# RWKV-7 chunk preparation: decay sums and head sums as products on the tensor engine instead of a scan and split operands

## The chip, the cores and the metric

The kernel runs on one core of a Trainium2 chip. The metric is the device time of one execution in microseconds (us), as the median of several runs. The engines are named as in the profile: PE is the tensor engine (PEld its weight loads), DVE the vector engine, ACT the scalar engine, POOL the general-purpose engine (GpSimd), and SP the engine whose queue issues most of the transfers.

## The reference, cut to what matters

The reference is a trunk of two layers on 1024 positions of 1024 channels, all in float32. The first layer (RG-LRU and HGRN2 beside each other) isn't touched. The second is RWKV-7 time mixing with 16 heads of 64 channels:

```
r, k, v, g = einsum("pbsd,pdw->pbsw", mixes[:4], w_in)
w_log = -softplus(-(w0 + tanh(mixes[4] @ w1) @ w2)) - 0.5
decay = exp(-exp(w_log))
iclr  = sigmoid(a0 + (mixes[5] @ a1) @ a2)
kk = heads(k * k_k);  kk = kk / max(norm(kk), 1e-12)
k  = heads(k * (1 + (iclr - 1) * k_a))
# step: state = state * w + (state @ -kk) (kk * iclr)^T + v k^T ;  y = state @ r
bonus = sum(r * k * r_k, axis=-1) * v
```

Two things of this matter here. The exponent of the decay is -exp(-0.5) times a sigmoid, so the decay over several positions is the exponential of a running sum of sigmoids. And two sums go over the 64 channels of a head: the squared norm of `kk`, and the sum of `r * k * r_k`.

## The kernel before, in words

The kernel works on the second layer in chunks of 64 positions. In a chunk the recurrence becomes products of matrices and the inverse of a triangular matrix of 64 x 64 per head. Three stages follow one another in time.

**Preparation** (`layer1_proj` from line 942 on, and `prep`, line 1144). The keys' projection runs over four units of weights (j), two halves of the positions (th, 512 each) and two column tiles of 128 channels (e2): sixteen slots, in the order of line 961. In each slot `dense_t` (lines 152 to 165) makes 24 products of 512 columns into a PSUM tile "mm". A generator `prep` for the same channels and half runs in three steps, one slot apart:

1. Two products per factor (lines 1152 to 1157) give the low-rank parts of decay and rate, channels on partitions, in PSUM tiles "l", of which there are two buffers. ACT takes the tanh of both (SG and IC, lines 1160 and 1161; the decay's constant w0 is the bias). DVE adds 1 (line 1166) and makes the running sum GC inside each chunk with a scan whose first factor `cst` is 0 at the start of a chunk (line 1167). ACT makes E1 and E2, the exponentials of plus and minus the sum (lines 1172 and 1174); E2 lies in the tile of SG. POOL makes the right half of AR (line 1176).
2. With the projected keys: KP and the square SQ, the scaled keys KK (lines 1181 to 1183); `head_sums` of SQ (line 1185) and of RK, which is r times k times r_k (line 1192); BT (line 1188), the left half of AR (line 1189) and KTt, which lies in the tile of GC (line 1194).
3. Sixteen small products (line 1201) into a tile "s", copied by ACT to AB (line 1205), and eleven transfers on SP's queue: AR, BT, KTt and AB to DRAM (lines 1206 to 1217).

`head_sums` (lines 1219 to 1228) splits its operand into two float32r parts (the high one by ACT, line 149; the low one by DVE, line 150) and multiplies both with a selector of 64 columns that puts the two heads' sums into their rows of one PSUM tile `nb` of 64 x 512, in which all the slots add. After the last slot `norms` (line 1230) copies `nb`, transposes the bonuses' part, and inverts the norms, on 32 partitions by 512 columns (line 1241); they go to DRAM in eight transfers (line 1245) and come back in two (line 1256), with 32 positions to a row.

**Values and inversions** (`chain_phase`, line 1023). The value pieces (`vpiece`, lines 1000 to 1011; their 24 products of 256 columns are lines 184 to 186) run on PE, six of them still before `chain_phase`; their mixes are made at the same time in the tiles "KK" of the preparation. The inversions (`invert`, line 1264) are long rows of small DVE steps (lines 1294 to 1306), which begin with a block of AB's products scaled by the inverse norms (lines 1275 to 1279, on POOL).

**The chunks** one after another (`gram`, `chain`, `norm`, `project`), with the other inversions, the gates and the output among them.

The order of the instructions on each engine isn't written out by hand. The program issues its steps in the order of the code above, and a scheduler that simulates the timeline when the kernel is built arranges them by priority and simulated readiness; each engine then runs its list in that order. Tiles of one name (or tag) share a fixed number of buffers, and a write waits for the last reader of the buffer's earlier tile.

Of the kernel before, what the change touches and what calls it, by code (L numbers as in the profile page):

```python
# [11 lines left out]
ALU = mybir.AluOpType  # L12
# [13 lines left out]
# columns of the packed per-channel vectors, eight columns each  # L26
# [6 lines left out]
class Steps:  # L33
    """a generator with the parts that it makes"""
# [11 lines left out]
class Net:  # L46
# [39 lines left out]
    # ---------------------------------------------------------------- constants  # L86
# [15 lines left out]
    def mask_from(self, pool, tmp, name, shape, conds):  # L102
        """uint8 mask, 1 where every affine condition (pattern, base, cm) >= 0 holds."""
# [48 lines left out]
    def dense_t2(self, w, e, uh, ul, th):  # L152
        """[128 channels, 512 positions] of unit w's e-th column tile, in two steps."""
# [21 lines left out]
    def dense_n(self, w, uh, ul, tt):  # L175
        """[128 positions, 256 channels] of unit w."""
# [12 lines left out]
    def rstd(self, pool, ss, n, scale, eps):  # L189
        """(ss * scale + eps) ** -0.5 on [128, n]."""  # L190
# [6 lines left out]
    def rstd2(self, pool, ss, n, scale, eps):  # L197
        """the same by the square root of the scalar engine and a Newton step"""
# [10 lines left out]
    def norm_rows(self, pool, x, sq):  # L209
        """root-mean-square scale [128,1] of a row tile [128, 1024]."""  # L210
        nc = self.nc
        ss = pool.tile([P, 1], F32, name="ss")
        nc.scalar.activation(sq, x, AF.Square, accum_out=ss)
        return self.rstd(pool, ss, 1, 1.0 / D, EPS)

    # ---------------------------------------------------------------- layer 0
    def layer0(self):
        tc, nc, a = self.tc, self.nc, self.a
        with ExitStack() as cx:
            uh, ul = ([[self.mx.tile([P, HALF], F32R, name=f"x{n}{th}") for _ in range(KT)] for th in range(2)] for n in "hl")  # L220
            rgk = cx.enter_context(self.pool("rgk", 1))
            with ExitStack() as c2:
# [38 lines left out]
                # the first projections of the next part lie in PSUM until its pools are there  # L261
# [17 lines left out]
    def warm(self, pool, n):  # L279
        """products of zeros that keep the tensor engine's clock up until there is work"""  # L280
# [9 lines left out]
    def hgrn_consts(self, c, hp):  # L290
        nc = self.nc
        # lower bound and its complement, per channel
# [16 lines left out]
        # masks of a 64-block's rows and columns, the same in both halves of the partitions  # L309
# [6 lines left out]
        # (block, group of blocks, source block of a group)  # L316
# [9 lines left out]
    def hgrn_dense(self, c, big, uh, ul, trees):  # L326
        """the projections, in pieces; a tree starts when its queries and keys are there"""
# [61 lines left out]
    def advance(self, gens):  # L389
        """a stage of the first tree, at times one of the second too"""  # L390
# [5 lines left out]
    def hgrn_half(self, hp, stp, th, j, tr, st, diag, lev):  # L396
        """two heads, four blocks of 128 positions each; the heads run in step"""
        nc = self.nc
        # scores, transposed
# [3 lines left out]
        def scores(i, rhs, w, n, b):  # L403
            """products of the sources of a block of 64 with its groups of n blocks of b targets, w blocks apart"""
# [9 lines left out]
        def put(i, ps, w, b, g, s, mask, dst, src):  # L414
            """the blocks dst of every group of g from the slots src of every w, where the mask allows it"""
# [9 lines left out]
        def wider(i, b, pool):  # L425
            """sources with their way through the other half of a block of 2 * b, totals of such blocks"""
# [8 lines left out]
        # positions themselves and next ones  # L435
# [17 lines left out]
        # blocks of 4 * b from such of b: the slots of a group are queries of its blocks 0 to 3 (even ones) and those of  # L453
        # blocks 2, 3, 3 with their ways through block 1, blocks 1 and 2, block 2 (odd ones)
# [57 lines left out]
        for Q, F, K, V, G, row in tr:  # L512
            # keys with positions on partitions
# [72 lines left out]
    def rglru(self, cx, uh, ul):  # L586
        tc, nc, a = self.tc, self.nc, self.a
        # -8 softplus(-lam) per channel: max(-lam, 0) + log1p(exp(-|lam|))
# [19 lines left out]
        # sigmoids by tanh: sigmoid(z) = (1 + tanh(z / 2)) / 2  # L608
# [11 lines left out]
        for j in range(4):  # L620
# [45 lines left out]
            # the halves of the two sigmoids that are factors, squared  # L666
# [10 lines left out]
    def out0(self, cx):  # L677
# [9 lines left out]
        for th in range(2):  # L687
# [69 lines left out]
    def finish(self, rp, th, Y, ss):  # L757
        """norms and residual of four row tiles, and their channels on partitions"""
# [29 lines left out]
    def receptance(self, w, j, th, e2):  # L788
        """a column tile of r, in two steps"""
# [15 lines left out]
    def mix_parts(self, mp, p, th, eng=None):  # L805
        """the same, a channel tile at a step"""
# [13 lines left out]
    def mixes(self, mp, p, th, eng=None):  # L820
        """the parts of one half of a mix, in the slots of that half"""
# [8 lines left out]
    def lora_consts(self):  # L830
        """the first factors of decay and rate, times 1 - mu and times mu"""
# [16 lines left out]
    def lora(self, th):  # L848
        """low-rank decay and rate of one half"""
# [18 lines left out]
    def lora_parts(self, th, x):  # L868
        """the low parts of the decays on the second half of the partitions, those of the rates on the first"""
# [7 lines left out]
    def layer1_consts(self):  # L877
# [6 lines left out]
        # halves for sigmoids by tanh: 1 + (sigmoid - 1) k_a = tanh * k_a / 2 + 1 - k_a / 2  # L884
        cols = lambda n: self.vec[:, VIDX[n]:VIDX[n] + KT]
        self.hw0, self.ha0, self.hka, self.omka = (c.tile([P, KT], F32, name=n) for n in ("hw0", "ha0", "hka", "omka"))
        nc.vector.tensor_scalar(self.hw0, cols("w0"), 0.5, None, ALU.mult)
# [4 lines left out]
    def layer1_proj(self):  # L892
# [7 lines left out]
        self.ddd = dt("ddd", [4, 16, 8, 32])  # L900
# [4 lines left out]
        with ExitStack() as cx:  # L905
            mp = self.mx
            with ExitStack() as c2:
                lp = c2.enter_context(self.pool("lora", 1))
                # parts of the low-rank factors: high ones twice, against the two parts of the other factor
                self.l2h = [lp.tile([P, D], F32R, name=f"l2h{i}") for i in range(2)]  # L910
                self.l2l = lp.tile([P, D], F32R, name="l2l")
                self.LT = [lp.tile([P, S], F32R, name=f"LT{i}") for i in range(2)]
                with ExitStack() as c3:
# [3 lines left out]
                    for i in range(2):  # L917
# [3 lines left out]
                        nc.gpsimd.tensor_sub(self.l2l[r], l2[r], self.l2h[i][r].bitcast(F32))  # L921
                    self.lora_parts(0, self.LT0)
# [19 lines left out]
                with ExitStack() as c3:  # L942
                    kp = c3.enter_context(self.pool("kp", 2))
                    # selectors that put a head's sum over its channels into its row: norms and bonuses, in them halves, in them heads
                    sel = kp.tile([P, 120], F32, name="SQ", bufs=1)
                    nc.gpsimd.memset(sel, 0.0)
                    for h in range(2):
                        nc.gpsimd.memset(sel[64 * h:64 * h + 64, 56 + 8 * h:57 + 8 * h], 1.0)
                    self.sel = kp.tile([P, 120], F32R, name="sel", bufs=1)
                    nc.gpsimd.tensor_copy(self.sel, sel)  # L950
                    cst = kp.tile([P, 8, 64], F32, name="cst", bufs=1)
                    nc.gpsimd.memset(cst, 1.0)
                    nc.gpsimd.memset(cst[:, :, 0:1], 0.0)
                    self.cst = cst
# [655 lines left out]
```

## Time and profile before

| | |
|---|---|
| median of 3 runs | 1878.74 us (1875.97, 1878.74, 1879.16) |
| span of the profiled execution | 1879.1 us (nothing is shown around the span) |
| PE busy | 1726.0 us, 92% |
| PEld busy | 1447.4 us, 77% |
| DVE busy | 1353.5 us, 72% |
| ACT busy | 767.7 us, 41% |
| POOL busy | 717.3 us, 38% |

Times of single instructions and of stretches come from that one profiled execution, and are us from the start of its span. A busy share of PE isn't PE at its peak, since products overlap in their durations: what a product costs in a row of products is read from the distance of their starts. An instruction line such as "L1167 DVE ... GC<-cst,SG" is line 1167 of the kernel; a helper's line, such as 150, stands for all that calls it, and the names of the tiles tell which call it was. In a group's line the numbers after the bar are busy us and the mean ns of one, then the engine's idle time before them and what ended it. In a line of the waits the numbers are us in total, how often, and the longest. A granted clock of 0.5 means that PE ran at half speed.

### The profile page before, as it was taken

To read this page: it belongs to the slowest core of one execution; us is meant where nothing else is said; L and a number is where in the kernel's file an instruction comes from. 1 tells how busy PE (TensorE), PEld (TensorE's weight loads), DVE (VectorE), ACT (ScalarE), POOL (GpSimd) and SP (SyncE) were. 2 spreads that over 40 slices of the span, in tenths; PEclk is the share of its full clock that TensorE was granted. 3 is DMA by queue.
4 is the path that set the end of the run, shared out by engine and by line. 5 is a ranking of instruction groups with operands and counts; after the bars stand their busy time and mean duration, and the time that the engine had idled before them with its cause. 6 is when DMAs were issued, how large, how long until landed. Compare 5 with 4: busy or idle time off the path is not lost. (4 is left out here: it accounts for less than half of the span.)

```text
span 1879.1 us, 34525 instructions
## 1 busy us (share of the span) xinstructions
PE 1726.0 (92%) x13394; PEld 1447.4 (77%) x13394; DVE 1353.5 (72%) x2621; ACT 767.7 (41%) x1468; POOL 717.3 (38%) x638
## 2 busy tenths in 40 slices
PE   7989989999899999999999999979788879978888
PEld 6879789787897777777878766669787868867666
DVE  6585483675847889745355686885999999489984
ACT  5322222323226755545454765666452223242221
POOL 5534232333222212465434243555532333373530
PEclk9989999999899999999999999969889889788989
DMA  5101101111022111375332266756344444664531
GB/s 182 46 24 46 56 18 63 46 35 39 19 72 86 50 63 67 124 236 173 101 123 96 90 152 155 176 138 188 101 144 130 141 129 136 181 197 146 163 102 62
DMA packets 177491, 201.79 MB, mean 107 GB/s; under 512 B 91440, under 2 KB 122416, under 8 KB 177328
## 3 DMA queue, kind: packets, MB, share of 16 engines
q1 hardware_dynamic: 176176, 195.39, 34.9%
q0 software_dynamic: 1152, 4.19, 0.7%
q8 instruction: 106, 1.74, 0.4%
q14 instruction: 57, 0.47, 0.1%
HBM read 136.28 MB, written 63.24 MB: 106 GB/s over the span
## 5 line engine op out<-in xcount | busy, mean ns | idle before, releaser
L135 POOL TENSOR_TENSOR wl<-w,wh 128x1024 fp32r<-128x1024 f32 x110 | 275.5, 2511 | 288.7 <-ACT wh L133 280.6
L160 PE MATMUL mm<-xh,wh 128*128 128x512 f32 x768 | 306.8, 400 | 1.4 <-ACT KK L1183 1.4
L162 PE MATMUL mm<-xh,wl 128*128 128x512 f32 x768 | 305.4, 398 | 0.0
L161 PE MATMUL mm<-xl,wh 128*128 128x512 f32 x768 | 304.6, 397 | 0.0
L184 PE MATMUL mm<-wh,xh 128*128 128x256 f32 x560 | 170.6, 305 | 6.0 <-ACT xh L149 4.4
L160 PEld LDWEIGHTS mm<-xh,wh 128*128 128x128 f32 x768 | 145.6, 190 | 37.0 <-issue 3.9
L162 PEld LDWEIGHTS mm<-xh,wl 128*128 128x128 f32 x768 | 146.0, 190 | 35.3 <-issue 5.0
L186 PE MATMUL mm<-wh,xl 128*128 128x256 f32 x560 | 167.5, 302 | 5.0 <-DVE xl L150 4.3
L161 PEld LDWEIGHTS mm<-xl,wh 128*128 128x128 f32 x768 | 145.9, 190 | 33.3 <-issue 3.4
L185 PE MATMUL mm<-wl,xh 128*128 128x256 f32 x560 | 166.3, 297 | 0.0
L133 ACT CAST wh<-w 128x1024 fp32r<-128x1024 f32 x112 | 117.3, 1049 | 115.8 <-PE mm L161 57.1
L1294 DVE TENSOR_TENSOR PR<-YP,BL 128x80 f32<-128x80 f32 (+20 forms) x240 | 125.8, 545 | 14.1 <-POOL BL L1276 12.0
L184 PEld LDWEIGHTS mm<-wh,xh 128*128 128x128 f32 x560 | 115.0, 205 | 9.7 <-ACT xh L149 5.0
L186 PEld LDWEIGHTS mm<-wh,xl 128*128 128x128 f32 x560 | 114.5, 206 | 7.2 <-DVE xl L150 5.4
L185 PEld LDWEIGHTS mm<-wl,xh 128*128 128x128 f32 x560 | 114.9, 205 | 0.7
L184 PE MATMUL po<-wh,xh 128*128 128x256 f32 x256 | 80.8, 316 | 1.3 <-DVE vg L1020 1.3
L1415 PE MATMUL pg<-GM,BK 64*128 64x128 f32 x512 | 64.3, 328 | 17.0 <-DVE RB L1421 11.5
L185 PE MATMUL po<-wl,xh 128*128 128x256 f32 x256 | 79.5, 311 | 0.0
L186 PE MATMUL po<-wh,xl 128*128 128x256 f32 x256 | 78.2, 306 | 0.0
L803 DVE SCALAR_TENSOR_TENSOR mix<-ut,vec,mix 128x512 f32<-128x512 f32 x64 | 57.2, 902 | 27.6 <-ACT mix L802 26.8
L420 DVE COPY_PREDICATED ST<-m_l,sm 64x128 f32<-64x128 uint8 x224 | 72.4, 337 | 5.5
L1415 PEld LDWEIGHTS pg<-GM,BK 64*128 64x128 f32 x512 | 52.5, 222 | 23.0 <-issue 19.0
(374 smaller groups left out, 4355.7 us busy)
## 6 DMA issues: line engine op xcount, KB each, us to landing
w<-in_W SPq DMA_DIRECT2D x112, 512.0 KB, 3.7
ard<-AR SPq DMA_DIRECT2D x16, 512.0 KB, 4.1
BK<-bkd SPq DMA_DIRECT2D x16, 512.0 KB, 4.2
vd<-vg SPq DMA_DIRECT2D x32, 256.0 KB, 2.9
GM<-ard SPq DMA_DIRECT2D x32, 256.0 KB, 4.4
x<-in_x SPq DMA_DIRECT2D x8, 512.0 KB, 10.1
mgd<-sgq SPq DMA_DIRECT2D x16, 256.0 KB, 2.3
ut<-mgd SPq DMA_DIRECT2D x16, 256.0 KB, 4.5
```

What stands on the lines that cost most here:

```text
L133: nc.scalar.copy(hi, w)
L135: (nc.vector if first else nc.gpsimd).tensor_sub(lo, w, hi.bitcast(F32))
L160: nc.tensor.matmul(ps, lhsT=wh[:, c:c + P], rhs=a, start=(k == 0), stop=False)
L161: nc.tensor.matmul(ps, lhsT=wh[:, c:c + P], rhs=b, start=False, stop=False)
L162: nc.tensor.matmul(ps, lhsT=wl[:, c:c + P], rhs=a, start=False, stop=(k == KT - 1))
L184: nc.tensor.matmul(ps, lhsT=a, rhs=h, start=(k == 0), stop=False)
L185: nc.tensor.matmul(ps, lhsT=a, rhs=l, start=False, stop=False)
L186: nc.tensor.matmul(ps, lhsT=b, rhs=h, start=False, stop=(k == KT - 1))
L420: nc.vector.copy_predicated(d, m, x)
L803: nc.vector.scalar_tensor_tensor(out, sh, self.v(f"mu{p}", k), out, ALU.mult, ALU.add)
L1294: nc.vector.tensor_mul(pr, fv(YP, yo, kd + [[48, 8], [1, n]]), fv(BL, ao + i, k0 + [[0, 8], [32, n]]))
L1415: nc.tensor.matmul(ps[h][:, q, :], lhsT=BK[hs, eg * 4 + q, :], rhs=GM[hs, h, eg * 4 + q, :], start=True, stop=True)
```

## The change

The decays' low-rank products are made for a pair of slots at once and the other way round, with positions on partitions (`decays`): the product's constant w0 comes in as one more product, of ones with two rows that hold its high and low parts. The tanh of them, SG, is the stationary operand of a product with a triangle of ones, which is zero between chunks; so the running sum GC comes out of PE, channels on partitions, in a PSUM tile "l". What the "+1" adds to the sum (the count of positions in the chunk) comes in as products of ones with `cnt`. The exponentials read GC from PSUM. E2 has buffers of its own, which AB uses after it, and KTt lies in the tile of KP.

A head sum is now a full float32 product without a split: each 128 positions of the operand are the stationary operand, and two columns that mark the two heads (`sel`) stream. So the sums come with positions on partitions, each at its own place of `nb`, and nothing is added up over slots. The bonuses need no transposition; the norms are inverted on 128 x 128, transposed once, stored in four transfers and loaded in eight.

```
+    def decays(self, kp, j, th):
+        nc, LT, cs = self.nc, self.LT[0], slice(j * 256, (j + 1) * 256)
+        SG = kp.tile([P, 4, 256], F32, name="SG")
+        ps = [self.pss.tile([P, 2, 256], F32, name="l") for _ in range(2)]
+        for i in range(3):
+            for q in range(4):
+                t = slice((th * 4 + q) * P, (th * 4 + q + 1) * P)
+                l, r = ((LT[:, t], self.l2h[0][:, cs]), (LT[0:64, t], self.l2l[0:64, cs]),
+                        (self.ones[0:64], self.w0r[:, cs]))[i]
+                nc.tensor.matmul(ps[q // 2][:, q % 2], lhsT=l, rhs=r, start=(i == 0 and q % 2 == 0), stop=(i == 2),
+                                 skip_group_check=True)
+        for i in range(2):
+            nc.scalar.activation(SG[:, 2 * i:2 * i + 2], ps[i], AF.Tanh, scale=0.5)
+        return SG
...
-        pw = self.pss.tile([P, HALF], F32, name="l")
-        nc.tensor.matmul(pw, lhsT=self.l2h[0][:, es], rhs=LT[0][:, sl], start=True, stop=False)
-        nc.tensor.matmul(pw, lhsT=self.l2l[0:64, es], rhs=LT[0][0:64, sl], start=False, stop=True)
...
-        nc.scalar.activation(SG, pw, AF.Tanh, scale=0.5, bias=self.hw0[:, e:e + 1])
...
-        nc.vector.tensor_scalar(SG, SG, 1.0, None, ALU.add)
-        nc.vector.tensor_tensor_scan(GC, cst.rearrange("p c t -> p (c t)"), SG, 0.0, ALU.mult, ALU.add)
+        GC = self.pss.tile([P, HALF], F32, name="l")
+        for q in range(2):
+            nc.tensor.matmul(GC[:, q * 256:(q + 1) * 256], lhsT=self.ones, rhs=self.cnt, start=(q == 0), stop=False,
+                             skip_group_check=True)
+        for q in range(4):
+            nc.tensor.matmul(GC[:, q * P:(q + 1) * P], lhsT=sg[:, q, e % 2 * P:(e % 2 + 1) * P], rhs=self.tri, start=False,
+                             stop=(q == 3), skip_group_check=True)
...
-        E2 = SG
+        E2 = t("E2")
...
-        KTt = GC
+        KTt = KP
...
-        AB = kp.tile([P, 8, 64], F32, name="AB")
+        AB = c3(E2)
...
-    def head_sums(self, kp, e, th, i, x):
-        hi, lo = (kp.tile([P, HALF], F32R, name=f"s{n}", bufs=1) for n in "hl")
-        self.split(x, hi, lo)
-        c = 56 - 32 * i - 16 * th - e
-        for p in (hi, lo):
-            nc.tensor.matmul(self.nb, lhsT=self.sel[:, c:c + 64], rhs=p,
...
+    def head_sums(self, e, th, i, x):
+        for q in range(4):
+            self.nc.tensor.matmul(self.nb[:, i, 4 * th + q, :, e], lhsT=x[:, 2 * q:2 * q + 2, :], rhs=self.sel,
+                                  start=True, stop=True)
...
     def norms(self, kp):
+        nc.scalar.copy(f(self.bon), f(self.nb[:, 1]))
+        T = kp.tile([P, 2, P], F32, name="T", tag="KK")
+        nc.vector.reciprocal(T[:, 0], f(self.nb[:, 0]))
+        nc.vector.tensor_scalar(T[:, 0], T[:, 0], 1e24, 0.5, ALU.min, ALU.mult)
+        ps = self.pss.tile([P, P], F32, name="s")
+        nc.tensor.transpose(ps, T[:, 0], self.ident)
+        nc.scalar.copy(T[:, 1], ps)
+        for ci in range(4):
+            nc.sync.dma_start(out=self.ddd[ci], in_=T[:, 1, ci * 32:(ci + 1) * 32])
...
+            for ci in range(4):
+                o = 64 * d + 16 * ci
+                nc.sync.dma_start(out=self.D[o:o + 16], in_=self.ddd[ci].rearrange("(a h) t -> h a t", h=16))
```

In `layer1_proj` the decays of the next pair of slots are issued after the first step of the pair's second slot, ahead of its projection; the first pair's are issued ahead of all slots. The constants (`prep_consts`, `w0r`) are made once, mostly on POOL, with two small transfers. The value pieces that are made before `chain_phase` take the tag "E2" in place of "AB". The rest of the diff takes out comments.

More of the change, by code (lines that the diff above doesn't have):

```diff
@@ L885, in layer1_consts @@
         cols = lambda n: self.vec[:, VIDX[n]:VIDX[n] + KT]
-        self.hw0, self.ha0, self.hka, self.omka = (c.tile([P, KT], F32, name=n) for n in ("hw0", "ha0", "hka", "omka"))
-        nc.vector.tensor_scalar(self.hw0, cols("w0"), 0.5, None, ALU.mult)
+        self.ha0, self.hka, self.omka = (c.tile([P, KT], F32, name=n) for n in ("ha0", "hka", "omka"))
         nc.vector.tensor_scalar(self.ha0, cols("a0"), 0.5, None, ALU.mult)
@@ L912, in layer1_proj @@
                 self.LT = [lp.tile([P, S], F32R, name=f"LT{i}") for i in range(2)]
+                self.w0r = lp.tile([64, D], F32R, name="w0r")
                 with ExitStack() as c3:
@@ L921, in layer1_proj @@
                         nc.gpsimd.tensor_sub(self.l2l[r], l2[r], self.l2h[i][r].bitcast(F32))
+                    b = self.mt.tile([P, D], F32, name="w0", tag="l2", bufs=1)
+                    nc.gpsimd.memset(self.w0r.bitcast(F32), 0.0)
+                    for r in (slice(0, 1), slice(32, 33)):
+                        nc.sync.dma_start(out=b[r], in_=a["w0r"])
+                        nc.gpsimd.tensor_copy(self.w0r[r], b[r])
+                    nc.gpsimd.tensor_sub(self.w0r[r], b[r], self.w0r[r].bitcast(F32))
                     self.lora_parts(0, self.LT0)
@@ L943, in layer1_proj @@
                     kp = c3.enter_context(self.pool("kp", 2))
[L945 to L954, printed above, removed]
+                    self.prep_consts(kp)
                     self.psd = c3.enter_context(self.pool("psd2", 3, space=PSUM))
                     self.pss = c3.enter_context(self.pool("pss2", 2, space=PSUM))
-                    self.nb = self.pss.tile([64, HALF], F32, name="n", bufs=1)
+                    self.nb = self.pss.tile([P, 2, 8, 2, KT], F32, name="n", bufs=1)
                     run = []
@@ L970, in layer1_proj @@
                             pk = []
-                            run.append(self.prep(kp, e, th, pk))
+                            run.append(self.prep(kp, e, th, pk, sg))
                             next(run[-1])
+                            if e2 == 1 and i < 7:
+                                sg = self.decays(kp, *order[i + 1])
                             pk.append(self.dense_t(w[j], e2, hi, lo, th))
@@ L1142, in output_weight, with prep_consts, prep @@
             self.W[2 * i + q, dh] = hi, lo
-    def prep(self, kp, e, th, pk):
+    def prep_consts(self, kp):
         nc = self.nc
-        LT, cst = self.LT, self.cst
+        self.sel = kp.tile([P, 2], F32, name="sel", bufs=1)
+        nc.gpsimd.memset(self.sel, 0.0)
+        for h in range(2):
+            nc.gpsimd.memset(self.sel[64 * h:64 * h + 64, h:h + 1], 1.0)
+        tri = self.tri = kp.tile([P, P], F32, name="tri", bufs=1)
+        nc.gpsimd.memset(tri, 1.0)
+        nc.gpsimd.affine_select(out=tri, in_=tri, pattern=[[1, P]], compare_op=ALU.is_ge, fill=0.0, base=0,
+                                channel_multiplier=-1)
+        nc.gpsimd.memset(tri[0:64, 64:128], 0.0)
+        self.ones = kp.tile([P, P], F32R, name="ones", bufs=1)
+        nc.gpsimd.memset(self.ones.bitcast(F32), 1.0)
+        one = kp.tile([P, 8, 64], F32, name="one", tag="KK")
+        cst = kp.tile([P, 8, 64], F32, name="cst", tag="KK")
+        nc.gpsimd.memset(one, 1.0 / 128)
+        nc.gpsimd.memset(cst, 1.0)
+        nc.gpsimd.memset(cst[:, :, 0:1], 0.0)
+        self.cnt = kp.tile([P, 256], F32R, name="cnt", bufs=1)
+        f = lambda x: x.rearrange("p c t -> p (c t)")[:, 0:256]
+        nc.vector.tensor_tensor_scan(self.cnt, f(cst), f(one), 0.0, ALU.mult, ALU.add)
+    def decays(self, kp, j, th):
[12 more added lines that the diff above has]
+        return SG
+    def prep(self, kp, e, th, pk, sg):
+        nc = self.nc
+        LT = self.LT
         sl = slice(th * HALF, (th + 1) * HALF)
@@ L1255, in invert_consts @@
         for d in range(2):
-            nc.sync.dma_start(out=self.D[64 * d:64 * d + 64], in_=self.ddd.rearrange("c h a t -> (c h) a t"))
+            for ci in range(4):
+                o = 64 * d + 16 * ci
+                nc.sync.dma_start(out=self.D[o:o + 16], in_=self.ddd[ci].rearrange("(a h) t -> h a t", h=16))
         self.YI = iv.tile([P, 8, 48], F32, name="YI", bufs=1)
@@ L1589, in pack @@
     arrays = {"x": f["x"][0], "W": W, "vec": vec, "gnorm": f["hg_out_norm"][0].reshape(P, 1),
-              "rg_w_a": f["rg_w_a"][0], "rg_w_x": f["rg_w_x"][0], "lora1": lora1, "lora2": lora2, "rows": rows, "ln": ln}
+              "rg_w_a": f["rg_w_a"][0], "rg_w_x": f["rg_w_x"][0], "lora1": lora1, "lora2": lora2, "w0r": f["rw_w0"][0].reshape(1, D), "rows": rows, "ln": ln}
     return {k: np.ascontiguousarray(v) for k, v in arrays.items()}
```

34 lines of the change are left out of this document (9 added, 25 removed).

## The prediction

> **What bounds the kernel now.** I read the table of windows first, to see which engine limits the stretch that the change edits. The columns are: start and end, length, then busy us and instructions of PE, PEld (weight loads), DVE, ACT and POOL, the granted PE clock, the DMA share and GB/s.
>
> ```profile
> span 1879.1 us, 34525 instructions
> ```
> ```profile
> 1060.00:1260.00 200.00, 183.34 (x1113) 129.86 (x1111) 161.59 (x174) 127.41 (x213) 96.29 (x92) 0.91 0.63 152
> 1220.00:1240.00 20.00, 13.23 (x70) 8.83 (x71) 18.66 (x20) 13.78 (x25) 14.33 (x14) 0.50 0.66 160
> 1240.00:1260.00 20.00, 16.59 (x132) 13.90 (x130) 17.72 (x17) 11.80 (x25) 11.07 (x7) 0.74 0.61 142
> 1300.00:1600.00 300.00, 255.09 (x3365) 234.86 (x3363) 289.33 (x659) 102.44 (x247) 113.79 (x84) 0.88 0.47 133
> ```
> The preparation of the chunks (sixteen slots, about 1060 to 1260) keeps PE busy for 183 of 200 us and DVE for 162. Near its end DVE is the fuller one, PE falls to 13 of 20 us and its clock to 0.50. From 1300 to 1600 DVE is full with the inversions, so what the change can move is the moment at which the first inversion starts. The chain of waits says what that moment hangs on (start, us, what):
>
> ```profile
> 1245.48 1.75 DVE sl L150
> 1261.06 0.21 PE mm L186
> 1271.29 0.83 ACT vg L1010 x4
> 1278.70 0.98 POOL YT L1252 x2
> 1293.62 2.33 DVE PR L1294
> ```
> It runs over a split of a head sum (DVE, line 150), then over PE's products of the value pieces, which queue behind all earlier products, and over short steps on ACT, DVE and POOL to the first inversion step at 1293.62. So before 1293 time is mostly PE's: what PE must do, and what it loses by waiting or at half clock. I take a shift of that moment as a shift of the whole time, since DVE is 96% busy behind it (289.33 of 300).
>
> How long a slot takes, and where PE waits in it:
>
> ```profile
> L1181 DVE TENSOR_TENSOR KP<-KP,mm x16: 661/684/690, 1077.3 to 1242.5; 128x512 f32<-128x512 f32 x16
> ```
> ```profile
> PE n L1226 <- DVE sl L150: 9.2, 4, 3.9
> PE n L1226 <- ACT sh L149: 3.8, 2, 2.2
> ```
> Fifteen steps from 1077.3 to 1242.5 are 11.0 us a slot. PE's waits of 13.0 us are for the two parts of the head sums' operand, which the change does away with.
>
> What PE does in a slot, from its timeline (start, us; the pitch is the distance of starts, since the durations overlap):
>
> ```profile
> 1126.53 0.40 PE L1226 MATMUL n<-sh,sel 128*64 128x512 f32 x1
> 1126.77 0.39 PE L161 MATMUL mm<-xl,wh 128*128 128x512 f32 x1
> 1127.00 0.40 PE L162 MATMUL mm<-xh,wl 128*128 128x512 f32 x1
> ...
> 1127.69 0.40 PE L1156 MATMUL l<-LT,l2h 128*128 128x512 f32 x1
> 1128.02 0.50 PE L1157 MATMUL l<-LT,l2l 64*128 64x512 f32 x1
> 1128.45 0.33 PE L1201 MATMUL s<-AR,IC 64*64 64x64 f32 x4
> 1128.71 0.45 PE L1226 MATMUL n<-sl,sel 128*64 128x512 f32 x1
> 1129.09 0.79 PE L1201 MATMUL s<-AR,IC 64*64 64x64 f32 x18
> 1129.86 0.45 PE L1226 MATMUL n<-sh,sel 128*64 128x512 f32 x1
> ...
> 1130.72 0.49 PE L1153 MATMUL l<-LT,l2h 128*128 128x512 f32 x1
> 1131.15 0.50 PE L1154 MATMUL l<-LT,l2l 64*128 64x512 f32 x1
> 1131.58 0.50 PE L162 MATMUL mm<-xh,wl 128*128 128x512 f32 x1
> ```
> The projection: 24 products at 0.23 us (1126.77 to 1127.00) = 5.5. The decay pair (L1153, L1154): 0.86. The rate pair (L1156, L1157): 0.76. Four head-sum products: 0.24 among the projection's (1126.53 to 1126.77), 0.38 elsewhere (1128.71 to 1129.09), by halves 4 x 0.31 = 1.24. The 32 records of L1201 at 0.043 (18 in 1129.09 to 1129.86) = 1.4. Sum 9.8 us. So a slot of 11.0 loses 1.2 us, over sixteen slots about 19.
>
> **The change, part by part.** *DVE.* Per slot it loses the "+1", the scan and two low parts:
>
> ```profile
> L1167 DVE TENSOR_TENSOR_SCAN GC<-cst,SG 128x512 f32<-128x512 f32 x16 | 28.2, 1762 | 0.6
> L150 DVE TENSOR_TENSOR sl<-SQ,sh 128x512 fp32r<-128x512 f32 x16 | 16.5, 1030 | 13.6 <-PE n L1226 8.2 <-ACT sh L149 5.4
> L1166 DVE TENSOR_SCALAR SG<-SG 128x512 f32<-128x512 f32 x16 | 15.7, 979 | 0.9 <-ACT SG L1160 0.9
> L150 DVE TENSOR_TENSOR sl<-R,sh 128x512 fp32r<-128x512 f32 x16 | 13.9, 871 | 3.5 <-PE n L1226 3.5
> ```
> That is 28.2 + 16.5 + 15.7 + 13.9 = 74.3 of its 161.6 us: DVE no longer limits any slot. ACT loses two casts a slot; its tanh keeps its 512 columns a slot; its two exponentials now read PSUM, which no row prices apart, and ACT, 64% busy, covers a few tenths either way. None of this is time won by itself: it is worth only what PE loses now.
>
> *PE, what goes:* the decay pair, 0.86, and four head-sum products, 1.24: 2.10 us a slot.
>
> *PE, what comes.* Rows of the same kinds of product:
>
> ```profile
> 535.32 1.05 PE L525 MATMUL sm<-V,KN 128*128 128x128 f32 x8
> 536.13 0.36 PE L184 MATMUL mm<-wh,xh 128*128 128x256 f32 x1
> ```
> ```profile
> 1258.44 0.43 PE L1237 MATMUL s<-ident,SQ 32*128 32x32 f32 x4
> ```
> ```profile
> 1264.24 0.28 PE L184 MATMUL mm<-wh,xh 128*128 128x256 f32 x1
> 1264.36 0.28 PE L185 MATMUL mm<-wl,xh 128*128 128x256 f32 x1
> ```
> ```profile
> L525 PEld LDWEIGHTS sm<-V,KN x128: 187/192/333, 127.6 to 539.4; 128*128 128x128 f32 x128
> ```
> A full-precision 128x128x128 product appears as two records (L525: 64 products in the code, 128 records), 8 of which take 0.81 us (535.32 to 536.13): 0.20 us a product. A float32r product of 256 columns has a pitch of 0.12.
> The decay products now give positions on rows: 12 of 256 columns per pair of slots, 12 x 0.12 = 1.44, plus the change to 64 rows and back, 0.30 (the rate pair's 0.76 less two full ones, 0.46): 0.87 a slot. Consecutive 64-row products in the same rows have no row; at the 0.2 that the second of a pair loses (0.43 less 0.23) for each of eight, the end is 1.6.
> The running sums: two products of ones by 256 columns, 0.24, and four full-precision products with the triangle, 0.80: 1.04 a slot.
> The head sums: eight full-precision products with two moving columns, sixteen records, each with a load of 128 columns. The nearest row in its small moving operand is L1237, four records with loads of 128 columns in 0.43 less a duration of 0.22, i.e. 0.07 each: 1.12. The nearest in kind is L525, 0.10: 1.6. A load that nothing overlaps lasts 0.19: 3.0. I take 0.07, since two columns are even less than L1237's 32.
> [...]
> Sum 0.87 + 1.04 + 1.12 = 3.03, net +0.93 a slot, +15 us over sixteen.
>
> *PE's losses.* Of the 19 us I expect 15 back: the head sums now wait for one ACT or DVE result each, DVE has slack, and PE, the only full engine, has the projection to fill with. The new product for the running sum waits only for a tanh computed slots earlier. Behind a late one stand the projection's products, and for them ACT and DVE.
>
> *The end of the stretch.* The split on the chain (1.75 us at 1245.48) goes, and the reciprocal shrinks:
>
> ```profile
> L1241 DVE RECIPROCAL SQ<-SQ 32x512 f32<-32x512 f32 x1 | 3.3, 3341 | 0.9 <-ACT SQ L1234 0.9
> ```
> From 512 columns to 128 it saves 2.5 us, ahead of the mixes. Against it, its tile now shares a tag with these mixes. I take 4 us off. The norms go out in 4 transfers in place of 8, and come back in 8 in place of 2, all on SP, with six more issues to be done before the first block of the inversions is scaled; the 15 us between POOL's YT and the first PR hold other steps of that scaling, so I price it at nothing, at worst about 3 us.
>
> *Waits that are added.* AB now lies in E2's buffers, so that the exponential two slots on waits for six transfers of AB:
>
> ```profile
> 1156.99 0.58 ACT L1205 COPY AB<-s 128x512 f32<-128x512 f32 x1
> ...
> 1159.94 0.45 SPq L1216 DMA_DIRECT2D a12d<-AB  x1
> ...
> 1163.44 0.61 ACT L1174 ACTIVATE SG<-GC 128x512 f32<-128x512 f32 x1
> ```
> The last issue is 3.5 us ahead of that exponential, so it is covered or nearly so. If it is late, ACT's queue behind it (the next squares and keys) and the bank of the running sum stand still; ACT has 36% free. Three PSUM tiles a slot instead of two share the two "l" banks: also a price that I put at zero, up to 1 us a slot if the banks are handed on late. The constants w0r and the triangle are made once on POOL, beside PE.
>
> *Sum.* +15 - 15 - 4 = -4 us against the profiled span of 1879.1 us, which gives 1875; that span is at the upper end of the three runs (median 1878.74), a difference below what matters here.
>
> **The rivals.** *Slower: the loads of the indicator products.* PE becomes the bound with nothing to hide the sixteen loads a slot. At 0.13 us a record (between 0.10 and 0.19) they cost 0.96 us a slot more than taken: +15, so 1890. It decides from 0.10 us on: 0.03 x 256 records = 8 us lift the sum from -4 to +4. For it: PE is busy in nearly all windows and the only engine that gets work. Against it: L1237.
> *Faster: PE's losses vanish.* All 19 us come back, the last forty microseconds run at full clock (0.50 and 0.74 now) for some 6 us more than taken: 15 - 19 - 10 = -14, 1865. For it: the waits of 13.0 us have their cause removed. Against it: other waits take their turn once the order is computed anew.
> *No effect.* If the instruction order, not DVE, makes the losses, and loads stay cheap, the terms cancel to within 0.2%, about 3.8 us, which is what a measurement of this kernel can tell from no change.
>
> **How the numbers follow.** The near-balance (1875, own range 1866 to 1884) gets 0.50, of which 0.22 falls faster by over 0.2%, 0.20 within, 0.08 slower. The loads get 0.33 (0.30 slower, 0.03 within). The vanishing losses get 0.17, all faster. Together faster 0.39, within 0.23, slower 0.38. The range reaches from 1858 (losses gone, and some 7 us of PE's additions cheaper) to 1898 (records at 0.16 us: 256 x 0.09 = 23 on the sum), which leaves out loads that overlap nothing at all and both new waits at their full price.
>
> **What would show it.** Right: DVE near 87 us in the stretch, no PE wait for line 150's splits, PE's clock near 1.0 up to 1260, a slot of 10.9 to 11.1 us, the first PR about 4 us earlier. The records of the indicator products 0.07 us apart decide between forecast and rival; 0.10 or more, and slots of 11.5 or longer, would make the prediction wrong. ACT waiting for AB's transfers, or PE for an "l" bank, would show a price that I put at zero.

## The result, and the profile after

The changed kernel takes 1899.33 us (median; 1896.63 to 1900.08), the kernel before 1878.95 beside it: a ratio of 1.0103, 95% interval 1.0079 to 1.0128. It is slower by 1.0%, 20 us; the prediction was 1875 with a range up to 1898. The profiled execution:

```profile
span 1897.0 us, 35264 instructions
```

The windows of after, the same stretches as in the prediction (start and end, length, busy us and instructions of PE, PEld, DVE, ACT and POOL, the clock, DMA share, GB/s):

```profile
1060.00:1260.00 200.00, 197.39 (x1419) 161.19 (x1419) 93.14 (x103) 102.52 (x165) 80.08 (x91) 0.96 0.59 141
1220.00:1240.00 20.00, 20.00 (x158) 15.99 (x158) 9.69 (x10) 13.29 (x22) 13.17 (x11) 1.00 0.68 162
1240.00:1260.00 20.00, 20.00 (x169) 16.99 (x168) 14.06 (x16) 12.41 (x20) 13.34 (x15) 1.00 0.80 193
1300.00:1600.00 300.00, 262.47 (x3351) 241.99 (x3351) 273.15 (x645) 107.45 (x268) 118.58 (x86) 0.89 0.46 135
```

DVE is relieved as forecast (93 us instead of 162), and the trough of PE from 1220 on is gone (20 of 20 us at full clock, where before showed 13.23 at 0.50). But PE is now full: 197 of 200 us. The key products of the slots, first in all sixteen slots, then in seven late ones:

```profile
L1222 DVE TENSOR_TENSOR KP<-KP,mm x16: 673/689/690, 1085.8 to 1261.5; 128x512 f32<-128x512 f32 x16
```
```profile
L1222 DVE TENSOR_TENSOR KP<-KP,mm x7: 686/687/689, 1165.7 to 1236.2; 128x512 f32<-128x512 f32 x7
```

The first one comes 8.5 us later than before (1085.8 against 1077.3). Of these, 2.1 us stand there already when the first decay product starts (1064.80 against 1062.74), and 6.4 us arise between it and the first key product (21.0 us against 14.5). The fifteen steps take 175.7 us instead of 165.2, and in the steady middle a slot is (1236.2 - 1165.7) / 6 = 11.75 us. PE's waits in the stretch, against 13.0 us for the splits before:

```profile
PE n L1263 <- DVE R L1232: 1.3, 2, 1.0
PE l L1179 <- ACT E L1215: 1.0, 1, 1.0
PE n L1263 <- ACT SQ L1223: 0.8, 1, 0.8
PE l L1204 <- ACT E L1215: 0.6, 1, 0.6
```

So PE waits for almost nothing, and the slot is still longer: it is PE's own work. Its timeline in one slot:

```profile
1165.53 0.33 PE L1242 MATMUL s<-AR,IC 64*64 64x64 f32 x4
1165.79 0.50 PE L1179 MATMUL l<-l2h,LT 128*128 128x256 f32 x2
1166.22 0.50 PE L1179 MATMUL l<-l2l,LT 64*128 64x256 f32 x2
1166.57 0.40 PE L1179 MATMUL l<-w0r,ones 64*128 64x256 f32 x2
1166.89 1.03 PE L1242 MATMUL s<-AR,IC 64*64 64x64 f32 x28
...
1171.14 0.95 PE L1263 MATMUL n<-sel,SQ 128*128 128x2 f32 x8
1171.95 1.03 PE L1263 MATMUL n<-sel,R 128*128 128x2 f32 x8
1172.85 0.48 PE L1204 MATMUL l<-cnt,ones 128*128 128x256 f32 x2
1173.16 1.05 PE L1207 MATMUL l<-tri,SG 128*128 128x128 f32 x8
1173.97 0.47 PE L161 MATMUL mm<-xl,wh 128*128 128x512 f32 x1
```

From starts to starts: the sixteen records of the head sums take 1.71 us (1171.14 to 1172.85), counts and triangle 1.12 (to 1173.97), six decay products 1.10 (1165.79 to 1166.89; twelve for two slots, so 1.10 a slot). The chain of waits at the end of the stretch:

```profile
1252.99 1.68 PE n L1263 x16
...
1276.82 1.50 DMA ddd<-T
...
1293.11 0.93 POOL YT L1284 x2
...
1305.47 2.36 POOL BL L1309
1307.96 2.33 DVE PR L1328
```

The sixteen records of the last head sums, the store of the norms, POOL's YT and the scaling of the first block (BL) lead to the first inversion step at 1307.96, 14.3 us later than before. Another 3.5 us are added behind it.

### The profile page after: what moved, and what is told of

The parts are those of the page before. It is cut to its first block, busy times and chain, and to the rows that moved or that the text cites. A ratio compares the mean times of both kernels' runs of the same rounds, so it can differ in the third digit from the quotient of the medians.

```text
span 1897.0 us, 35264 instructions
## 1 busy us (share of the span) xinstructions
PE 1749.5 (92%) x13807; PEld 1485.9 (78%) x13807; DVE 1282.6 (68%) x2557; ACT 752.2 (40%) x1437; POOL 719.0 (38%) x646
## 4 chain that ended last, share of the span: by engine, by line
PE 53%; DVE 30%; DMA 6%; issue 4%; POOL 3%; ACT 2%; SPq 2%; DVEq 0%; POOLq 0%; ACTq 0%
PE mm L160 7%; PE mm L162 7%; PE mm L161 7%; DVE PR L1328 4%; DVE ST L420 3%; PE mm L186 2%; PE mm L184 2%; PE mm L185 2%; DMA yn<-yd 2%; DVE YP L1331 2%; DVE PR L1337 1%; PE n L1263 1%; PE sm L720 1%; PE sm L721 1%; PE sm L722 1%
## 5 line engine op out<-in xcount | busy, mean ns | idle before, releaser
L1328 DVE TENSOR_TENSOR PR<-YP,BL 128x48 f32<-128x48 f32 (+14 forms) x240 | 125.0, 543 | 21.0 <-POOL BL L1310 15.3
L1222 DVE TENSOR_TENSOR KP<-KP,mm 128x512 f32<-128x512 f32 x16 | 11.0, 687 | 89.9 <-issue 65.4
## 6 DMA issues: line engine op xcount, KB each, us to landing
x<-in_x SPq DMA_DIRECT2D x8, 512.0 KB, 10.3
```

The lines of the kernel that those rows point to most:

```text
L1328: nc.vector.tensor_mul(pr, fv(YP, yo, kd + [[48, 8], [1, n]]), fv(BL, ao + i, k0 + [[0, 8], [32, n]]))
```

## The experiments

Each was timed beside the kernel before; its ratio goes to that, since the kernel before itself had medians of 1879.8 to 1885.6 in the groups of runs. "First solve" is the first PR step. It comes from the one profiled execution of each run, while a ratio rests on several executions of both kernels.

**Parts alone.** First the bonus sums were left out of the changed kernel (what reads them then takes the norms' sums, so the output isn't the reference's):

```
-        self.head_sums(e, th, 1, c3(RK))
-        nc.scalar.copy(f(self.bon), f(self.nb[:, 1]))
+        nc.scalar.copy(f(self.bon), f(self.nb[:, 0]))
```

> The changed kernel without the head sums of r times k times r_k: eight records' worth of half the indicator products a slot are left out, 128 of 256 records (the bonuses take the norms' sums instead, so the bonus part of the output isn't the reference's). Theory 'PE is the bound and each load of 128 columns costs its time' (0.105 us a record in the changed kernel's trace): 8 x 0.105 = 0.84 us a slot, 13 us over sixteen slots, so about 1886 us, some 14 us under the changed kernel's 1899. Rival 'waits': the added waits (AB in E2's buffers, the two l banks, T among the mixes) make the loss and PE fills them anyway: within 4 us of 1899.

1889.87 us, 1.0046 (1.0027 to 1.0064). The slot:

```profile
L1222 DVE TENSOR_TENSOR KP<-KP,mm x7: 687/687/689, 1166.2 to 1231.6; 128x512 f32<-128x512 f32 x7
```

10.9 us a slot instead of 11.75: 0.85 us for eight records, 0.106 each. The first solve came 12 us earlier, and by the ratios (1.0103 to 1.0046) the kernel got 0.6% faster, about 11 us. The profiled execution itself was the slowest of this run's twelve (1898.33 us), so its time behind the first solve, 600.7 us, isn't typical of the kernel. The range of the rival, within 4 us of 1899, wasn't met.

Then only the new head sums and norms, in the kernel before; and only the decays with the running sums, in the kernel after with the old head sums (and one buffer for SG in place of two, for room):

```
-        SG = kp.tile([P, 4, 256], F32, name="SG")
+        SG = kp.tile([P, 4, 256], F32, name="SG", bufs=1)
```

> The kernel before with the new head sums and norms alone; decays by scan as before. Theory 'PE is the bound': PE gets 16 x 0.105 = 1.68 us a slot for 1.24, +7 us in all, DVE loses 30 us of splits and PE's waits of 13 us for them; the sum is near or a little below before: 1868 to 1880. Rival 'waits': neither E2 nor the l banks are touched, so the full relief shows: below 1868.

> The changed kernel with the old head sums (split, 64-column selector) and old norms; the decay sums by products stay. (SG has one buffer instead of two, for room.) Theory 'PE is the bound': PE gets 2.2 us a slot of decay products, counts and triangle for 0.86, +22 us in all, and the losses by the splits stay: 1888 to 1898, most of the 20 us. Rival 'waits': as slow as the changed kernel or slower, 1897 to 1903. If the head sums were what costs: 1879 or below.

1880.43 us, 1.0005 (0.9988 to 1.0023), and 1880.47 us, 1.0001 (0.9985 to 1.0017): each part alone changes nothing, both together cost 1%. The heads alone show what their relief of DVE is worth in a slot:

```profile
L1179 DVE TENSOR_TENSOR KP<-KP,mm x8: 686/687/687, 1122.8 to 1195.0; 128x512 f32<-128x512 f32 x8
```

10.3 us a slot (72.2 / 7), less than the 11.0 of before, and just the prediction's 9.8 with 1.71 in place of 1.24 for the head sums: nothing is lost in it. The gain was gone again by the first solve (1293.9): the first decay product came 3.0 us later than before, and the end of the stretch took 4.2 us longer. The decays alone missed the ranges of both theories. Their slots are longer than before:

```profile
L1224 DVE TENSOR_TENSOR KP<-KP,mm x7: 675/687/689, 1164.3 to 1235.6; 128x512 f32<-128x512 f32 x7
```

That is 11.9 us a slot (71.3 / 6). Their first solve came 5.3 us later than before, at 1298.9, and the time behind it was 6 us shorter (579.4 against 585.5). So the heads alone fit into the 1.2 us a slot that PE lost before. The decays alone don't: their loss is made up behind the first solve, in an order of steps that differs. That the two parts together cost 1% because PE has no idle time left for both is my reading of this.

**More of PE's work without the decays.** The kernel of the heads alone with each product of a head sum issued twice:

```
+            for _ in range(2):
                 self.nc.tensor.matmul(self.nb[:, i, 4 * th + q, :, e], lhsT=x[:, 2 * q:2 * q + 2, :], rhs=self.sel,
```

> The kernel before with the new head sums and norms alone (the kernel of the earlier run that changed nothing), each of the head sums' products issued twice into the same place (the same values). TensorE gets 1.68 us a slot more than with them once, so about +34 us of products in the stretch against before, more than the change's own +29, but without a running sum, without the three-part decays and without their waits for the PSUM banks called l. Theory 'TensorE is full': before it had about 19 us of waits and some half-clock time in the sixteen slots, and what goes beyond that shows: 1893 to 1903, first pair of solves at 1305 to 1312. Rival 'the waits of the decays' (late start by the l banks, T in the keys' buffers): the cost belongs to the decays, so no more than 1888, with the first key product at 1078 to 1081.

1909.1 us, 1.0133 (1.01 to 1.0166), above both ranges, and far above that of the rival, which puts the cost on the decays; the first solve came at 1329.6. The stretch:

```profile
1060.00:1260.00 200.00, 200.00 (x1265) 158.78 (x1264) 106.47 (x118) 92.50 (x146) 63.80 (x73) 0.85 0.48 123
```

PE is busy in 200 of 200 us, and yet its clock is 0.85, the lowest of all the kernels. Behind the first four steps the shortest slots take 12.1 us, 1.8 more than with the sums once, which is their records; the longest take 14.7. I read this as a double cost of the products of two columns, their loads and the clock. The second half of it rests on the count at the end of this document.

**Less of PE's work.** The one-buffer kernel as a control, then two edits that take products away, one in this control and one in the kernel after. Folding puts the bias into the other half of the rows of the low product, so that eight products of 128 rows do what twelve did (LX holds the high part of LT in its first 64 rows and ones in the others; w0r the low part of the weights and the bias rows):

```
-        for i in range(3):
+        for i in range(2):
...
-                l, r = ((LT[:, t], self.l2h[0][:, cs]), (LT[0:64, t], self.l2l[0:64, cs]),
-                        (self.ones[0:64], self.w0r[:, cs]))[i]
+                l, r = ((LT[:, t], self.l2h[0][:, cs]), (self.LX[:, t], self.w0r[:, cs]))[i]
```

The other, in the kernel after, drops the counts:

```
+            nc.vector.tensor_scalar(SG[:, 2 * i:2 * i + 2], SG[:, 2 * i:2 * i + 2], 1.0, None, ALU.add)
...
-            nc.tensor.matmul(GC[:, q * 256:(q + 1) * 256], lhsT=self.ones, rhs=self.cnt, start=(q == 0), stop=False,
```

> The kernel after with one buffer in place of two for the decays' tanh (SG), which the decays-only run had for room. A control: if that run gained by it, this one is faster than after by several us; both theories expect no gain, 1897 to 1903 (slower if the single buffer makes the next decays' tanh wait).

> The kernel of the one-buffer control with the bias row folded into the low product: eight products of 128 rows for a pair of slots in place of twelve, four of them of 64 rows each before. Takes about 6 us of products out of the stretch (four of twelve by 1.1 us for six, eight pairs) plus the changes between 64 and 128 rows. 'TensorE is full': 6 us or more below the control. 'The waits of the decays': the banks are held through one group of products less, but no more than 2 us. 'The order of the later work decides': any sign, by up to 10 us, with the first solve earlier by 5.

> The kernel after with the two count products of each slot (0.31 us) taken away and a one added to the decays' tanh by VectorE instead (two instructions of 512 elements for two slots). 5 us of TensorE's work less, about 9 us of VectorE's more in a stretch where VectorE is idle a third of the time. 'TensorE is full': 1892 to 1896. 'The waits of the decays': the running sums wait for VectorE too, so 1899 or more.

The control took 1899.22 us, 1.0071 (1.0055 to 1.0087), the same time as after (1899.33), beside a slower run of the kernel before. Without the counts the kernel after was at 1905.42 us, 1.0106 (1.0077 to 1.0135): no gain, although 5 us of PE's work are gone. PE waited 2.7 us for SQ and the clock was 0.95. The folded kernel took 1876.86 us, 0.9958 (0.9943 to 0.9972): 22 us less than the control, nearly three times the products that it takes away, and faster than the kernel before. Its decay products, and its stretch:

```profile
1218.98 0.50 PE L1183 MATMUL l<-l2h,LT 128*128 128x256 f32 x2
1219.32 0.39 PE L1183 MATMUL l<-w0r,LX 128*128 128x256 f32 x2
1219.64 0.56 PE L1246 MATMUL s<-AR,IC 64*64 64x64 f32 x12
```
```profile
1060.00:1260.00 200.00, 197.60 (x1534) 165.78 (x1533) 99.58 (x116) 112.86 (x190) 90.38 (x97) 1.00 0.64 151
```

Four products take 0.66 us here and 0.56 in the other slot of a pair, instead of 1.10 and 1.08 for six; over the sixteen slots the decays' products take 9.4 us instead of 17.1 in the control. The clock is 1.00 through the whole stretch instead of 0.95 in the control, by my estimate worth about 200 x 0.05 = 10 us more. Another part of the 22 us isn't the folding: this kernel has its rows of ones ready before the stretch, the control hasn't.

**Number or rows.** The folded kernel with its second product issued twice, each time with the values of the moving operand halved, so that the sum is the same: twelve products again, all of 128 rows.

```
+                    nc.gpsimd.tensor_scalar(self.w0r, self.w0r.bitcast(F32), 0.5, None, ALU.mult)
...
+        for i in range(3):
...
+                l, r = ((LT[:, t], self.l2h[0][:, cs]), (self.LX[:, t], self.w0r[:, cs]))[min(i, 1)]
```

> The folded kernel with its second product issued twice with halves of its moving rows (the same sum): twelve products for a pair of slots as in the kernel after, but all of 128 rows. In the traces six of them with rows of 64 among them took 1.10 us (after), four of 128 rows 0.56 (folded). If it is the number of products that costs, six of 128 rows take 0.80 to 0.85, the slot 11.5, the time 1884 to 1890. If the 64 rows and the changes to and from them cost, they take 0.8 as well but the clock keeps full as in the folded kernel: 1878 to 1883. If the later order decides, up to 1900 with the first solve under 1297.

> The folded kernel with the count products taken away and the one added on VectorE: 0.31 us of TensorE's work a slot less, 5 us in all. 'TensorE is full': 1870 to 1875, slot near 11.0. With the wait for VectorE that it puts ahead of the running sums, and the half clock that came with it in the earlier run of this edit: 1878 or more.

1878.76 us, 0.9993 (0.9972 to 1.0013) with twelve full products, 0.35% above the folded kernel's ratio, with intervals that touch: the number costs little, at most. Six of them took 0.89 us (1221.13 to 1222.02) or 0.80, 13.5 us over all slots, where the folded kernel's took 9.4; the slot was 11.44, the clock 0.98:

```profile
1221.13 0.50 PE L1184 MATMUL l<-l2h,LT 128*128 128x256 f32 x2
1221.47 0.63 PE L1184 MATMUL l<-w0r,LX 128*128 128x256 f32 x4
1222.02 0.92 PE L1247 MATMUL s<-AR,IC 64*64 64x64 f32 x24
```

The folded kernel without the counts took 1873.58 us, 0.9967 (0.9949 to 0.9986), not to be told from the folded one by its ratio, though its slot is 11.06 us against 11.27.

**Rows or the late first decays.** The kernels with LX had their ones early. In the kernel after, ones are made inside the stretch, and PE's order has the first bias products 14 us behind the other ones; until then the first decays hold both "l" tiles:

```profile
1065.36 0.73 PE L1179 MATMUL l<-l2l,LT 64*128 64x256 f32 x4
1079.42 0.73 PE L1179 MATMUL l<-w0r,ones 64*128 64x256 f32 x4
```

Two runs cross the two: 64 rows with early ones, and folded products with late ones.

```
+                self.on0 = lp.tile([64, P], F32R, name="on0")
+                nc.gpsimd.memset(self.on0.bitcast(F32), 1.0)
...
-                        (self.ones[0:64], self.w0r[:, cs]))[i]
+                        (self.on0, self.w0r[:, cs]))[i]
```
```
-                nc.gpsimd.memset(self.LX[64:128].bitcast(F32), 1.0)
...
+        nc.gpsimd.tensor_copy(self.LX[64:128], self.ones[64:128, 0:1].broadcast_to([64, S]))
```

> The one-buffer control with the 64 rows of ones that the bias products multiply in a tile of their own, made before the stretch (in the kernel after they are made on GpSimd at 1068.5, after the first decays' other products, and the bias products of the first decays come 14 us later, at 1079.4, so that these decays hold both l banks until then). The products keep their 64 rows. 'Late start': the first decays are whole at 1066, the first slots run earlier and more at full clock, and most of the 20 us between the control (1899) and the run with twelve products of 128 rows (1879) is this: 1878 to 1886. 'The 64 rows cost': slot still 11.75, no more than 4 us won: 1895 or more.

> The folded kernel with its rows of ones copied from the tile made in the stretch, so that its second products of the first decays are as late as in the kernel after, with all products still of 128 rows and eight for a pair. 'Late start': 1889 to 1899, near the control, although its slot stays 11.25. 'The 64 rows cost': 1875 to 1880.

1893.88 us, 1.0065 (1.0041 to 1.0088) with 64 rows and early ones; 1883.17 us, 1.0015 (0.9999 to 1.0031) with folded products and late ones. Both lie between the ranges of the two theories. By the ratios, folding gives 1.1% with early ones (1.0065 to 0.9958) and 0.6% with late ones (1.0071 to 1.0015); early ones give 0.6% to the folded kernel and nothing that can be told to the one with 64 rows. Folding changes the number and the rows at once. The rows by themselves stand between two runs with early ones and twelve products each: 1.0065 with 64 rows among them, 0.9993 with 128 rows throughout, 0.7% or some 13 us, with intervals apart. The decays' products themselves account for 4 of these (17.5 us over all slots against 13.5); the clock in the stretch was 0.93 against 0.98, worth some 10 us by the same estimate as above. Why half clock came with the one and not with the other, no run shows.

What the late ones cost at the start is clear in the traces. From the first decay product to the first key product it takes 14.5 us before and 15.0 with the heads alone; 20.4 to 21.0 in every kernel with the new decays and late ones; 16.6 to 16.9 in the four with early ones. So 4 us of the late start come from the late ones, and some 2 from the rest of the new decays. The kernel with 64 rows and early ones won these 4 us and lost them again in the next slots: it ran most of a slot at half clock, where the one with twelve products of 128 rows kept full clock (this one's line is the second),

```profile
1098.00:1118.00 20.00, 20.00 (x93) 16.45 (x92) 4.34 (x6) 7.95 (x13) 7.30 (x7) 0.51 0.60 134
1098.00:1118.00 20.00, 20.00 (x164) 16.85 (x165) 8.66 (x9) 11.87 (x19) 11.99 (x10) 1.00 0.76 176
```

with PE busy all the time in both. The rows are the larger cause, the late ones the smaller.

**Buffers.** AB in the keys' buffers, the norms in a tile of their own, and AB in buffers of its own (the last two against the one-buffer control):

```
-        AB = c3(E2)
+        AB = c3(KK)
```
```
-        T = kp.tile([P, 2, P], F32, name="T", tag="KK")
+        T = kp.tile([P, 2, P], F32, name="T", bufs=1)
```
```
-        AB = c3(E2)
+        AB = kp.tile([P, 8, 64], F32, name="AB")
```

> The changed kernel with AB in KK's tile, which is free a whole slot earlier, instead of E2's: the second exponential no longer waits for the transfers of AB (18.9 us of waits on ACT in the changed kernel). Theory 'PE is the bound': ACT's waits were covered, within 4 us of 1899. Rival 'waits': 1885 to 1892.

> The one-buffer control with a tile of its own for the inverse norms, which in the kernel after lies in the keys' buffers beside the value mixes. The forecast took 4 us off the end of the stretch, and the traces of after and of the heads alone do not show them. If the shared buffers took them back, the time from the last product of the stretch (line of the s products) to the first solve goes from 38.5 to 35 or less and the total to 1894 to 1896; if the transfers of the norms and the value pieces set it, nothing changes (1897 to 1901).

> The one-buffer control with two buffers of its own for AB, as in the kernel before, in place of E2's. In the kernel after ScalarE waited 18.9 us, seven times, for the last transfer out of AB before the next exponential into the same buffer. 'The wait for AB's transfers' (priced at nothing in the prediction): the waits go, and with them the half clock in the first slots, 1885 to 1893. 'TensorE is full': the waits lie beside its work, 1896 to 1901, slot still 11.7.

AB in the keys' buffers: 1912.92 us, 1.018 (1.0152 to 1.0208), slower than after and outside both ranges. The wait moves to the keys, and at the end the chain runs through it:

```profile
1270.69 1.64 DMA a12d<-KK
1272.59 0.70 ACT KK L1224
```

The tile for the norms: 1897.03 us, 1.0086 (1.0059 to 1.0113), no change against the control's 1.0071. But the time from the last small product to the first solve did go down, from 38.5 to 32.4 us, which is what the theory of the shared buffers named; in all other traces it is 36.3 or more. The first solve came 6.4 us earlier than the control's, and behind it DVE had a long wait for the values' transfer:

```profile
DVE PR L1328 <- DMA SV<-vd: 11.4, 1, 11.4
```

AB apart: 1889.64 us, 1.0043 (1.0022 to 1.0063), within the first theory's range and 0.3% under the control's 1.0071 (1.0055 to 1.0087); the two intervals overlap a little. The wait that goes, as it stands in the kernel after:

```profile
ACT E L1215 <- DMA a12d<-E: 18.9, 7, 5.0
```

But the mechanism that I had put there isn't what the trace shows: the clock in the stretch fell from 0.95 to 0.91, the first solve was 5 us later than the control's, and the gain lies behind it (575 us from first solve to the end, against 592). So the wait was there, 18.9 us of ACT's time, against the prediction's "covered or nearly so". Whether it costs the kernel anything, 0.3% at most, these runs don't show.

## Why the prediction was wrong

**The head sums' records: the step that failed first.** I took 0.07 us a record from the row of four transposes (L1237), and left the row of the same kind of product, L525 with 0.10, to the rival. The trace has 0.107 (1.71 / 16), leaving out eight gave 0.106. That is 0.59 us a slot more than taken, 9 us. My row was of another kind of load: in the profiles a transpose's load lasts 0.14 us, with 32 rows (L1237 before) as with 128 (L1275 after), and the loads of L525 and of the head sums last 0.19. That the kernel's time hangs on these records is shown by the run without half of them, 0.6% faster, and by the run with twice as many, 1.0133 against 1.0005. The rival "loads of the indicator products" fits the trace: PE busy for 197 of 200 us, and 0.107 us a record where it decides from 0.10 on. Whether a record's load or the rest of it takes these 0.107 us, no run separates.

**The decays: 0.87 a slot taken, 1.10 measured.** The upper end, 0.2 us lost by each 64-row product, was 1.6 a slot (by its own terms 1.5); six products, four of them of 64 rows, took 1.10 us instead of 0.87, another 4 us. With all products of 128 rows six of them took 0.80 to 0.91. The running sums were near (1.12 for 1.04). With these three sizes the slot comes out as 9.8 + 0.93 + 0.59 + 0.23 + 0.08 = 11.6; the trace has 11.75.

**PE's losses: 15 us expected back.** The waits did go, from 13.0 to 3.7 us. But I took half clock for a result of waiting, and expected a full clock once PE is full. The clock in the stretch went from 0.91 only to 0.96, and the doubled head sums had 0.85 with no idle time at all. In the steady slots the term itself held: with the sizes above the change adds 1.83 us a slot, and a slot went from 11.0 to 11.75, so 1.1 of the 1.2 us came back. What stayed lost lies in the first slots (the fourth step took 16.6 us). I also didn't see that the first decays would wait for their ones and hold both "l" tiles until 1079.4. The making of the constants and the sharing of these tiles were prices that I put at zero: by the kernels with early ones, the two together are 4 us of the 8.5 by which the first key product is late.

**The end of the stretch: -4 us expected, +0.5 found** (last small product to first solve, 38.5 us against 37.9). The split and the reciprocal did go from the chain; the chain of after shows the norms' store in their place. I had set the tag that the norms' tile shares with the value mixes against this without a price: with a tile of its own the time is 32.4 us, so the sharing can have taken back all of it. That run's steps also come in another order, so the two aren't separated. The six more issues, too, were priced at nothing; the eight loads of the norms are issued from 1286.34 to 1291.34, where before two were issued within 1.1 us. No run changes them alone.

**The added-up sum.** To the first solve: 8.5 late start (2.1 of them ahead of the first decay product), 10.5 over fifteen steps, -5.2 between the last key product and the last small product, 0.5 behind it: 14.3 us. A further 3.5 us come behind it. I had taken a shift of the first solve as a shift of the whole; that holds only to about 10 us. From first solve to end it was 585.5 us before, 589.0 after, 592.4 in the control and 575.0 with AB apart, with the same code in that part, mostly in other orders. Each is one execution, and the executions of one kernel differ by up to 17 us (1881 to 1898 without the bonus sums), so how much of this is the order stays open, and with it the sizes of single experiments below some 0.3%.

**What was right:** DVE's relief (93 us, 87 forecast), the end of the splits' waits, and that PE would be the bound; and the signs named for its being wrong, records at 0.10 or more and slots of 11.5 or longer, are what the trace shows.

## What to carry to other kernels

Before work is moved to an engine that is 92% busy, price each new product by a row of its own kind: here a product with two moving columns took 0.107 us a record, and the row of its kind, with 0.10, was at hand. Fold small operands into full 128 rows, and have constants ready before the first product that needs them: here the two together turned a kernel 0.7% slower than before into one 0.4% faster (1.0071 to 0.9958). And look at what a full engine is full of: here 33 of 37 steps of 3.41 us with fewer than 2,500 moving columns were followed by half clock, and PE busy for 200 of 200 us went with a clock of 0.85.

## What the hardware showed that I had not expected

The granted clock changed in steps of 3.41 us: in the traces of before and after every stretch at one clock, but for the last, is a whole multiple of it long, at 1.0 or at 0.5. I counted, in the sixteen traces and between 1050 and 1315 us, the moving columns of all products that start in such a step at full clock (a step of projection products has 7,680, 15 of 512). Of the steps with fewer than 2,500 columns 33 of 37 were followed by half clock, of those from 2,500 to 3,300 30 of 77, of those above 5 of 997. So in this kernel half clock followed few streamed columns, with waits of PE (13.0 us in the stretch before, clock 0.91) and without (the doubled head sums, busy for 200 of 200 us, clock 0.85). That the columns are the cause is read from this count; no run changed them alone.

Products of 256 columns with 64 rows behind one another took 0.32 to 0.35 us a pair (after, 1166.22 to 1166.57 and on to 1166.89), those of 128 rows in the run with twelve 0.28 (four in 1221.47 to 1222.02), with a further 0.1 where the rows change (1165.79 to 1166.22, 0.43 for the first pair, against 0.34 in the folded kernel).
